# A two-layer trunk on one core: sums of h's blocks between the plain products, and the second product's pools laid out anew

## The chip, the cores and the metric

The kernel runs on one core of a Trainium2 chip. The core has five engines with a queue of instructions each: TensorE (PE: matrix products; its weight loads are listed as PEld), VectorE (DVE), ScalarE (ACT), GpSimd (POOL) and SyncE (SP, which here only issues transfers). Each queue runs in order; the engines wait for each other by semaphores. Transfers between memory and the on-chip SBUF run on 16 DMA engines, which the queues of SP and POOL feed. The metric is the device time of one execution in microseconds.

## The reference

One sequence of 1024 tokens, width 1024, two layers. Each layer modulates its input with a shift, scale and gate worked out from a vector c ("adaLN"), applies a token mixer, and then an MLP with squared ReLU:

```python
for i in range(DEPTH):                       # 2 layers
    mod = c_act @ ada_w[i] + ada_b[i]        # adaLN: 6 x 1024 columns
    shift_t, scale_t, gate_t, shift_c, scale_c, gate_c = ...
    h = rmsnorm(x, norm_g[i, 0]) * (1.0 + scale_t) + shift_t
    y = gla_mixer(h, ...) if i == 0 else diff_mixer(h, ...)
    x = x + gate_t * y
    h = rmsnorm(x, norm_g[i, 1]) * (1.0 + scale_c) + shift_c
    y = jnp.square(jax.nn.relu(h @ mlp_w1[i])) @ mlp_w2[i]   # 1024 -> 4096 -> 1024
    x = x + gate_c * y
return rmsnorm(x, final_g)
```

Layer 0 mixes with gated linear attention, layer 1 with differential softmax attention. All numbers are float32.

## The kernel before

Activations lie transposed: features on the 128 partitions, tokens in the free dimension, which is cut into two halves of 512 tokens. `x[k][half]` is block k (of 8) of the residual, `h[k][half]` the normed block. A float32 product is done in three passes: `split` (L113) makes a rounded copy `hi` on ScalarE (L114) and the rest `lo` on VectorE (L115), and `mm3` (L117) issues hi x hi, hi x lo and lo x hi. So every weight and every block of h costs one cast and one subtraction, and a block of 128 x 512 outputs from 1024 inputs is 24 matmuls.

A layer's second part is `stretch`, which runs `inner` (L762) and then `outer` (L908).

`inner` does the output projection, adds it to x, norms it, and then the MLP's first product. Output columns come in blocks n of 128. Blocks 0 to 3 are done plainly, for half 0 and then half 1 (L788 to L794): 24 matmuls, a squared ReLU (`squared`: L755 on ScalarE, L757 on VectorE), and a store to `hs` in memory (L760, issued by SP). Behind them stand the "sums of h's blocks" (L799 to L815). The remaining 28 blocks are done two at a time by `pair` (L855) with seven products instead of eight: h is seen as a 2 x 2 grid (blocks 0 to 3 and 4 to 7, half 0 and half 1), and four of the products take sums of its quarters. The sums are four VectorE subtractions for each k (L803 to L806) and four splits, three into tiles `tq` and the last (for product 4) into tiles of h. The weights of a pair are loaded as `raw` (L830) and `raw2` (L831); `ws` are their sums (L835 to L840), each split again. `part`, `sum`, `inner` are the tiles in which the products are put together (L862, L871).

`outer` is the MLP's second product, in eight parts c of 512 inner rows. A part has its weights, eight tiles `inner` loaded back from `hs` by `load_inner` (L926) and split, 12 matmuls for each of the 8 x 2 output blocks, and a residual add into x (L718). Before it all of x is loaded again (`load_x`, L728). In layer 0 it also works out the adaLN of layer 1: `ada_products` (L208) loads eight pieces of 256 KB (issued by POOL, L213; three buffers `ada_raw`) and accumulates them on VectorE (L216, L218) in one of two buffers `ada_acc`; in the next part `ada_sums` (L222) transposes them on TensorE (L226) and reduces them (L229). Twelve such products are needed, two are issued in each of the parts 0 to 5.

The order of the instructions on each engine is set by the framework's scheduler from the program and its dependences; only inside the two mixers is TensorE's order written out. On SP and on POOL transfers keep the order in which they are scheduled. Tiles come from pools that are stacked from the left or the right end of SBUF; with `reuse_waits="tile"` a new tile waits only for the tiles whose space it takes. Where a pool lies therefore decides what its first loads wait for: `raw2` and `ws` stand in the pool `st1`, over tiles of x that the sums read; the x of `outer` stands on the right, over `st1`; and the first tiles of layer 1's attention (`qk`, `v`, L1027) stand on the right, over that x.

Of the kernel before, what the change touches and what calls it, by code (L numbers as in the profile page):

```python
# [10 lines left out]
F32 = mybir.dt.float32  # L11
F32R = mybir.dt.float32r
# [4 lines left out]
ALU = mybir.AluOpType  # L17
# [4 lines left out]
P = 128  # L22
D = 1024
T = 1024
KT = D // P
HT = 512
# [56 lines left out]
def trunk(ctx: ExitStack, tc, a, out):  # L83
    nc = tc.nc
    pe, act, dve, pool = nc.tensor, nc.scalar, nc.vector, nc.gpsimd
# [5 lines left out]
    hp = ctx.enter_context(tc.tile_pool(name="hp", bufs=2 * KT))  # L91
# [3 lines left out]
    xs = dram.tile([KT, P, T], F32, name="xs")  # L95
# [17 lines left out]
    def split(hi, lo, src):  # L113
        act.copy(out=hi, in_=src)  # L114
        dve.tensor_tensor(out=lo, in0=src, in1=hi.bitcast(F32), op=ALU.subtract)  # L115
# [21 lines left out]
    def wcols(w, c0, n, pinned=False):  # L137

        return weight(w.rearrange("(k p) n -> p k n", p=P)[:, :, c0:c0 + n], [P, KT, n], pinned)
# [102 lines left out]
    def gla_v(hd, i, pinned=False):  # L242
# [12 lines left out]
    h = [[(hp.tile([P, HT], F32R, name="h_hi", tag="hhi"), hp.tile([P, HT], F32R, name="h_lo", tag="hlo"))]  # L255
         for _ in range(KT)]
# [6 lines left out]
    with tc.tile_pool(name="xa", bufs=4, reuse_waits="tile") as xa, \  # L263
# [47 lines left out]
        for j in range(4):  # L311
            t = xa.tile([P, D], F32, name="xt", tag="xt")
# [8 lines left out]
        for blk in range(4):  # L321
            c0 = blk * 256
            acc = pro2.tile([P, 2, 256], F32, name="acc", tag="acc")
            for kq in range(2):
# [3 lines left out]
                for i in range(4):  # L328
                    k = 4 * kq + i
# [23 lines left out]
            st = gp2.tile([P, 4], F32, name="st", tag="tr", bufs=2)  # L353
# [30 lines left out]
    with gla as g:  # L384
# [292 lines left out]
        h = new_h()  # L677
# [44 lines left out]
    def load_x(x, xp, halves, queue=nc.sync):  # L722
        for half in reversed(halves):
            for k in range(KT):
                x[k][half] = xp.tile([P, HT], F32, name=f"x{k}_{half}")
        for half in halves:
            for k in range(KT):
                queue.dma_start(out=x[k][half], in_=xs[k, :, half * HT:(half + 1) * HT])  # L728
# [33 lines left out]
    def inner(l, h, w_o, x, early, g, sm, tp, ps, acc_tile):  # L762
# [20 lines left out]
        h = h2  # L783

        w1 = a["mlp_w1"][l]
        ws = [wcols(w1, n * P, P) for n in range(4)]
        for half in range(2):
            for n in range(4):  # L788
                pt = acc_tile()
                for k in range(KT):  # L790
                    mm3(pt, ws[n][0][:, k, :], ws[n][1][:, k, :], *h[k][half], k == 0, k == KT - 1)
                r = tp.tile([P, HT], F32, name="relu", tag="t")
                squared(r, pt, True)
                store_inner(n, half, r)  # L794


        K2 = KT // 2
        ops = {1: [h[k][0] for k in range(K2)], 2: [h[k + K2][0] for k in range(K2)],
               3: [h[k + K2][1] for k in range(K2)], 4: [], 5: [], 6: [], 7: []}  # L799
        for k in range(K2):  # L800
            x11, x12, x21, x22 = x[k][0], x[k][1], x[k + K2][0], x[k + K2][1]
            t3 = tp.tile([P, HT], F32, name="t3", tag="t")
            dve.tensor_tensor(out=t3, in0=x22, in1=x12, op=ALU.subtract)  # L803
            dve.tensor_tensor(out=x12, in0=x12, in1=x11, op=ALU.subtract)
            dve.tensor_tensor(out=x22, in0=x22, in1=x12, op=ALU.subtract)
            dve.tensor_tensor(out=x21, in0=x21, in1=x22, op=ALU.subtract)  # L806
            for n, src in ((6, x22), (5, x12), (7, t3), (4, x21)):
                if n == 4:
                    t = (hp.tile([P, HT], F32R, name="h_hi", tag="hhi"), hp.tile([P, HT], F32R, name="h_lo", tag="hlo"))
                else:  # L810
                    t = [tq.tile([P, HT], F32R, name="tq", tag=f"t{n}{i}") for i in range(2)]
                split(t[0], t[1], src)
                ops[n].append(t)
        px.close()
        if early:  # L815
            early.close()
        st = g.enter_context(tc.tile_pool(name="st1", bufs=2, side="right", reuse_waits="tile"))

        def part(raw, shape):
# [5 lines left out]
        def pair_weights(n):  # L825

            src = w1.rearrange("(k p) n -> p k n", p=P)
            r1 = wraw.tile([P, KT, P], F32, name="raw", tag="raw")
            r2 = st.tile([P, KT, P], F32, name="raw2", tag="raw2")
            nc.sync.dma_start(out=r1, in_=src[:, :, n * P:(n + 1) * P])  # L830
            nc.sync.dma_start(out=r2, in_=src[:, :, (n + 1) * P:(n + 2) * P])  # L831
            lo_, hi_ = slice(0, K2), slice(K2, KT)
            x0 = part(r1, [P, KT, P])
            sa = st.tile([P, KT, P], F32, name="ws", tag="ws")
            dve.tensor_tensor(out=sa[:, hi_], in0=r2[:, lo_], in1=r2[:, hi_], op=ALU.add)  # L835
            dve.tensor_tensor(out=sa[:, lo_], in0=sa[:, hi_], in1=r1[:, lo_], op=ALU.subtract)
            x1 = part(sa, [P, KT, P])
            sb = st.tile([P, KT, P], F32, name="ws", tag="ws")
            dve.tensor_tensor(out=sb[:, lo_], in0=r1[:, lo_], in1=r2[:, lo_], op=ALU.subtract)
            dve.tensor_tensor(out=sb[:, hi_], in0=r1[:, hi_], in1=sa[:, lo_], op=ALU.subtract)  # L840
            x2 = part(sb, [P, KT, P])
            x3 = part(r2[:, hi_], [P, K2, P])
            return {1: (x0, 0), 2: (x0, K2), 6: (x1, 0), 5: (x1, K2), 7: (x2, 0), 3: (x2, K2), 4: (x3, 0)}
# [63 lines left out]

    def outer(l, ada_todo, after, g, tp, ps, acc_tile):  # L908

        xp = g.enter_context(tc.tile_pool(name="xp", bufs=1, side="right", reuse_waits="tile"))  # L910
        hid = g.enter_context(tc.tile_pool(name="hid", bufs=4, reuse_waits="tile"))
        sg = g.enter_context(tc.tile_pool(name="sg", bufs=3 if ada_todo else 5, reuse_waits="tile"))
        ga = g.enter_context(tc.tile_pool(name="ga2", bufs=2, reuse_waits="tile")) if ada_todo else None
        sm = g.enter_context(tc.tile_pool(name="sm2", bufs=2, reuse_waits="tile"))
        x = [[None, None] for _ in range(KT)]
        load_x(x, xp, range(2))
        add = residual(l, x)
        w2 = a["mlp_w2"][l]
        parts = FF // 512

        def load_inner(c):
            hd = [[None, None] for _ in range(4)]
            for half in range(2):
                for f in range(4):
                    raw = sg.tile([P, HT], F32, name="inner", tag="inner")
                    nc.sync.dma_start(out=raw, in_=hs[4 * c + f, :, half * HT:(half + 1) * HT])  # L926
                    if c % 2:
                        t = [hid.tile([P, HT], F32R, name="hd", tag=f"hd{half}{i}") for i in range(2)]
                    else:
                        t = [hp.tile([P, HT], F32R, name=f"h_{n}", tag=f"h{n}") for n in ("hi", "lo")]  # L930
                    split(t[0], t[1], raw)
                    hd[f][half] = t
            return hd

        sums = []
        hd = load_inner(0)
        for c in range(parts):
            ws = [weight(w2.rearrange("(f p) n -> p f n", p=P)[:, 4 * c:4 * c + 4, n * 256:(n + 1) * 256],
                         [P, 4, 256]) for n in range(4)]
            last = c == parts - 1  # L940
            now, hd = hd, None if last else load_inner(c + 1)
            for half, cols in ((0, slice(0, HT)), (1, slice(0, 256)), (1, slice(256, HT))) if last else \
                    ((0, slice(0, HT)), (1, slice(0, HT))):
                w = cols.stop - cols.start
                finish = after(half, cols, x, tp, sm, ps, acc_tile) if last else None
                for n in range(KT):
                    pt = acc_tile()[:, :w]
                    wh, wl = ws[n // 2]
                    c0 = (n % 2) * P
                    for f in range(4):  # L950
                        pe_last = mm3(pt, wh[:, f, c0:c0 + P], wl[:, f, c0:c0 + P],
                                      *(t[:, cols] for t in now[f][half]), f == 0, f == 3)
                    if half and n < len(sums):
                        with tc.issue_after(pe_last.ins):
                            ada_sums(*sums[n], ps)
                    add(n, half, pt, cols, 5)
                    if last and n == 4:
                        next(finish)
                for _ in finish or ():
                    pass  # L960
            sums = [(*todo, 512, ada_products(*todo, 512, ga, ga, pool, 2)) for todo in ada_todo[:2]]
            del ada_todo[:2]
            assert not (c >= parts - 2 and ada_todo)

    h1 = []
# [393 lines left out]
```

## Time and profile before

| | |
|---|---|
| time, median of 3 runs | 2523.32 us (2523.2 to 2525.15) |
| the profiled execution | 2523.76 us |
| its span in the profile | 2522.0 us |
| mean granted clock of TensorE | 0.977 |
| busy: PE, PEld, DVE | 2390.8 us (95%), 2055.2 (81%), 1679.3 (67%) |
| busy: ACT, POOL | 993.2 (39%), 200.5 (8%) |
| chain that ended last | PE 68%, issue 17%, DVE 7%, DMA 5%, ACT 3% |

The span is the time from the first to the last instruction that the profiler saw; the execution's own time holds a little more at its ends. Busy shares are over the whole span, though the stages have different limits. The granted clock is the share of TensorE's full clock (2.4 GHz) that it was given; 0.5 is 1.2 GHz. A wait is the idle time of an engine in front of an instruction, put down to what released it last.

### The profile page before, as it was taken

The numbers are of one execution on the slowest core, as the hardware profiler recorded it, in microseconds if no ns is written. First come the engines' busy times: TensorE is split into PE (matmuls) and PEld (weight loads), VectorE is DVE, ScalarE is ACT, GpSimd is POOL, SyncE is SP. The second block draws the span as 40 slices with busy tenths as digits, with TensorE's granted clock in tenths as the row PEclk, the third lists the DMA queues.
The fourth block names the chain that finished last, engine by engine and source line by source line (L and its number), as shares of the span: only waits on it lengthen the run. The fifth ranks groups of instructions, "written<-read, shape, count | busy, mean of one in ns | idle before, by whom it ended". The sixth has DMA issues, their size and how long they took to land.

```text
span 2522.0 us, 33385 instructions
## 1 busy us (share of the span) xinstructions
PE 2390.8 (95%) x12215; PEld 2055.2 (81%) x12215; DVE 1679.3 (67%) x3191; ACT 993.2 (39%) x1969; POOL 200.5 (8%) x354
## 2 busy tenths in 40 slices
PE   6899999979999899999899999999969999999998
PEld 5688878867888688888799999987758888788887
DVE  7777767657665576775587787788666665655444
ACT  5655555433333221212455555564443333322111
POOL 2011100000000111210121121110000000000000
PEclk8999999999999899999899999999989999999999
DMA  8333354514333755641111111024514333833211
GB/s 287 121 109 117 105 159 131 158 46 122 117 100 101 267 190 174 212 155 61 59 49 39 36 34 34 24 88 128 157 56 124 101 116 101 275 101 98 71 54 67
DMA packets 270116, 286.57 MB, mean 114 GB/s; under 512 B 15546, under 2 KB 200032, under 8 KB 269952
## 3 DMA queue, kind: packets, MB, share of 16 engines
q1 hardware_dynamic: 255552, 240.24, 29.9%
q0 software_dynamic: 12992, 41.97, 5.2%
q8 instruction: 96, 1.57, 0.3%
q10 hardware_dynamic: 1408, 2.24, 0.2%
q14 instruction: 68, 0.56, 0.1%
HBM read 222.52 MB, written 61.87 MB: 113 GB/s over the span
## 4 chain that ended last, share of the span: by engine, by line
PE 68%; issue 17%; DVE 7%; DMA 5%; ACT 3%; POOL 0%; SPq 0%; DVEq 0%; POOLq 0%; ACTq 0%
PE acc L119 12%; PE acc L118 12%; PE acc L120 12%; PE acc L851 3%; PE acc L853 3%; PE acc L852 3%; DMA ada_raw<-in_ada_w 3%; PE pp L118 3%; PE pp L120 3%; PE pp L119 3%; PE pr L118 1%; PE pr L119 1%; ACT et L1107 1%; PE pr L120 1%; PE at L1137 1%
## 5 line engine op out<-in xcount | busy, mean ns | idle before, releaser
L114 ACT CAST whi<-raw 128x1024 fp32r<-128x1024 f32 (+3 forms) x217 | 209.0, 965 | 485.1 <-PE acc L119 249.7
L718 DVE SCALAR_TENSOR_TENSOR x<-acc,mod,x 128x512 f32<-128x512 f32 (+1 forms) x312 | 222.5, 720 | 218.5 <-PE acc L120 217.5
L118 PE MATMUL acc<-h_hi,whi 128*128 128x512 f32 x896 | 353.1, 395 | 7.1 <-ACT h_hi L114 4.2
L119 PE MATMUL acc<-h_lo,whi 128*128 128x512 f32 x896 | 352.0, 393 | 6.3 <-DVE h_lo L115 6.3
L120 PE MATMUL acc<-h_hi,wlo 128*128 128x512 f32 x896 | 351.3, 393 | 0.0
L115 DVE TENSOR_TENSOR wlo<-raw,whi 128x1024 fp32r<-128x1024 f32 (+3 forms) x217 | 243.0, 1121 | 82.9 <-ACT whi L114 79.2
L118 PE MATMUL acc<-hd,whi 128*128 128x512 f32 (+1 forms) x576 | 211.8, 368 | 1.2 <-DVE x L718 1.2
L119 PE MATMUL acc<-hd,whi 128*128 128x512 f32 (+1 forms) x576 | 210.7, 366 | 0.0
L120 PE MATMUL acc<-hd,wlo 128*128 128x512 f32 (+1 forms) x576 | 210.6, 366 | 0.0
L118 PEld LDWEIGHTS acc<-h_hi,whi 128*128 128x128 f32 x896 | 169.3, 189 | 44.0 <-ACT h_hi L114 6.1
L119 PEld LDWEIGHTS acc<-h_lo,whi 128*128 128x128 f32 x896 | 169.7, 189 | 42.1 <-DVE h_lo L115 8.2
L120 PEld LDWEIGHTS acc<-h_hi,wlo 128*128 128x128 f32 x896 | 169.7, 189 | 35.3
L118 PE MATMUL pp<-whi,h_hi 128*128 128x384 f32 x512 | 184.0, 359 | 6.2 <-DVE v L115 6.2
L851 PE MATMUL acc<-h_hi,whi 128*128 128x512 f32 x448 | 175.2, 391 | 0.0
L852 PE MATMUL acc<-h_lo,whi 128*128 128x512 f32 x448 | 175.2, 391 | 0.0
L853 PE MATMUL acc<-h_hi,wlo 128*128 128x512 f32 x448 | 174.0, 389 | 0.0
L120 PE MATMUL pp<-whi,h_lo 128*128 128x384 f32 x512 | 173.6, 339 | 0.0
L119 PE MATMUL pp<-wlo,h_hi 128*128 128x384 f32 x512 | 173.3, 338 | 0.0
L851 PE MATMUL acc<-tq,whi 128*128 128x512 f32 x336 | 132.0, 393 | 38.0 <-ACT whi L114 38.0
L213 POOL DMA_DIRECT2D ada_raw<-in_ada_w x160 | 85.9, 537 | 985.3 <-PE acc L853 488.8
L218 DVE SCALAR_TENSOR_TENSOR ada_acc<-ada_raw,cact,ada_acc 128x512 f32<-128x512 f32 x140 | 104.8, 749 | 49.8 <-DMA ada_raw<-in_ada_w 48.7
L853 PE MATMUL acc<-tq,wlo 128*128 128x512 f32 x336 | 131.6, 392 | 0.1
(1800 smaller groups left out, 5188.8 us busy)
## 6 DMA issues: line engine op xcount, KB each, us to landing
raw<-in_mlp_w SPq DMA_DIRECT2D x128, 512.0 KB, 4.4
ada_raw<-in_ada_w POOLq DMA_DIRECT2D x160, 256.0 KB, 3.4
inner<-hs SPq DMA_DIRECT2D x128, 256.0 KB, 3.9
hs<-inner SPq DMA_DIRECT2D x112, 256.0 KB, 2.5
x<-xs SPq DMA_DIRECT2D x64, 256.0 KB, 5.8
raw<-in_gla_w_in SPq DMA_DIRECT2D x24, 512.0 KB, 3.9
xs<-x SPq DMA_DIRECT2D x48, 256.0 KB, 2.6
raw<-in_diff_w_in SPq DMA_DIRECT2D x64, 192.0 KB, 2.8
```

The costliest lines, as they stand in the source:

```text
L114: act.copy(out=hi, in_=src)
L115: dve.tensor_tensor(out=lo, in0=src, in1=hi.bitcast(F32), op=ALU.subtract)
L118: pe.matmul(out=o, lhsT=lh, rhs=rh, start=start, stop=False)
L119: pe.matmul(out=o, lhsT=lh, rhs=rl, start=False, stop=False)
L120: return pe.matmul(out=o, lhsT=ll, rhs=rh, start=False, stop=stop)
L213: queue.dma_start(out=w, in_=a["ada_w"][l].rearrange("(k p) n -> p k n", p=P)[:, k:k + kk, c0:c0 + n])
L218: dve.scalar_tensor_tensor(out=acc, in0=w[:, j, :], scalar=cact[:, k + j:k + j + 1], in1=acc, op0=ALU.mult, op1=ALU.add)
L718: return dve.scalar_tensor_tensor(out=t, in0=psum, scalar=mcols(l, gate)[:, kt:kt + 1], in1=t, op0=ALU.mult, op1=ALU.add)
L851: pe.matmul(out=pt, lhsT=lh, rhs=rh, start=begin and k == 0, stop=False, skip_group_check=True)
L852: pe.matmul(out=pt, lhsT=lh, rhs=rl, start=False, stop=False, skip_group_check=True)
L853: pe.matmul(out=pt, lhsT=ll, rhs=rh, start=False, stop=k == K2 - 1, skip_group_check=True)
L1107: act.activation(out=et[:, n * HT:n * HT + wn], in_=p[:, :wn], func=AF.Exp, bias=nm, scale=DH ** -0.5, accum_out=ssum[:, s, n:n + 1])
```

## The change

1. The sums of block k (three of its four splits with them) become a function, `sums_of`, called ahead of the plain product k of half 1. The splits for product 4 stay behind the plain products.
2. `raw2` and `ws` move to a pool `sw` of their own, which lies under `st1`.
3. In `outer`, x moves to the left side, and the adaLN tiles and the loads of `inner` to the right, over `sw` and `st1`. The x tiles are loaded between the two halves of part 0's inner tiles, behind the part's weights.
4. The adaLN products are issued as 0, 3, 3, 2, 2, 2, 0, 0 in parts 0 to 7, not 2, 2, 2, 2, 2, 2, 0, 0.

```diff
         for half in range(2):
             for n in range(4):
+                if half:
+                    sums_of(n)
                 pt = acc_tile()
...
+        def sums_of(k):
+            x11, x12, x21, x22 = x[k][0], x[k][1], x[k + K2][0], x[k + K2][1]
+            t3 = tp.tile([P, HT], F32, name="t3", tag="t")
+            dve.tensor_tensor(out=t3, in0=x22, in1=x12, op=ALU.subtract)
+            dve.tensor_tensor(out=x12, in0=x12, in1=x11, op=ALU.subtract)
+            dve.tensor_tensor(out=x22, in0=x22, in1=x12, op=ALU.subtract)
+            dve.tensor_tensor(out=x21, in0=x21, in1=x22, op=ALU.subtract)
+            for n, src in ((6, x22), (5, x12), (7, t3)):
+                t = [tq.tile([P, HT], F32R, name="tq", tag=f"t{n}{i}") for i in range(2)]
+                split(t[0], t[1], src)
+                ops[n].append(t)
...
         for k in range(K2):
-            for n, src in ((6, x22), (5, x12), (7, t3), (4, x21)):
...
+            t = (hp.tile([P, HT], F32R, name="h_hi", tag="hhi"), hp.tile([P, HT], F32R, name="h_lo", tag="hlo"))
+            split(t[0], t[1], x[k + K2][0])
+            ops[4].append(t)
...
+        sw = g.enter_context(tc.tile_pool(name="sw", bufs=2, side="right", reuse_waits="tile"))
         st = g.enter_context(tc.tile_pool(name="st1", bufs=2, side="right", reuse_waits="tile"))
...
-            r2 = st.tile([P, KT, P], F32, name="raw2", tag="raw2")
+            r2 = sw.tile([P, KT, P], F32, name="raw2", tag="raw2")
...
-        xp = g.enter_context(tc.tile_pool(name="xp", bufs=1, side="right", reuse_waits="tile"))
+        xp = g.enter_context(tc.tile_pool(name="xp", bufs=1, reuse_waits="tile"))
...
+        ga = g.enter_context(tc.tile_pool(name="ga2", bufs=2, side="right", reuse_waits="tile")) if ada_todo else None
+        sg = g.enter_context(tc.tile_pool(name="sg", bufs=3 if ada_todo else 5, side="right", reuse_waits="tile"))
...
-        load_x(x, xp, range(2))
...
+        def load_inner(c, between=lambda: None):
             hd = [[None, None] for _ in range(4)]
             for half in range(2):
+                if half:
+                    between()
...
+            if c == 0:
+                hd = load_inner(0, lambda: fetch_x(0))
+                fetch_x(1)
...
-            sums = [(*todo, 512, ada_products(*todo, 512, ga, ga, pool, 2)) for todo in ada_todo[:2]]
-            del ada_todo[:2]
+            n = (0, 3, 3, 2, 2, 2, 0, 0)[c]
+            sums = [(*todo, 512, ada_products(*todo, 512, ga, ga, pool, 2)) for todo in ada_todo[:n]]
+            del ada_todo[:n]
```

What this does to the order shows at three places. The first is VectorE in layer 0 at the end of the plain products (x_0 and x_1 are half 0 and half 1 of blocks of h; the last digits tell blocks apart). Before:

```order
L115 TENSOR_TENSOR h_lo<-x_1_4432,h_hi 128x512
L757 SCALAR_TENSOR_TENSOR relu<-relu 128x512 x5
L803 TENSOR_TENSOR t_5423<-x_1_4429,x_1_4425 128x512
L757 SCALAR_TENSOR_TENSOR relu<-relu 128x512
L804 TENSOR_TENSOR x_1_4425<-x_1_4425,x_0_4433 128x512
L115 TENSOR_TENSOR tq<-t_5423,tq 128x512
L805 TENSOR_TENSOR x_1_4429<-x_1_4429,x_1_4425 128x512
L115 TENSOR_TENSOR tq<-x_1_4425,tq 128x512
L806 TENSOR_TENSOR x_0_4437<-x_0_4437,x_1_4429 128x512
L115 TENSOR_TENSOR tq<-x_1_4429,tq 128x512
L803 TENSOR_TENSOR t_5444<-x_1_4430,x_1_4426 128x512
```

After, from the seventh relu of the plain products to just behind the eighth (lines L795 to L798 are the former L803 to L806):

```order
L757 SCALAR_TENSOR_TENSOR relu<-relu 128x512
L796 TENSOR_TENSOR x_1_4428<-x_1_4428,x_0_4436 128x512
L115 TENSOR_TENSOR h_lo<-x_0_4437,h_hi 128x512
L797 TENSOR_TENSOR x_1_4432<-x_1_4432,x_1_4428 128x512
L115 TENSOR_TENSOR tq<-x_1_4428,tq 128x512
L798 TENSOR_TENSOR x_0_4440<-x_0_4440,x_1_4432 128x512
L115 TENSOR_TENSOR tq<-x_1_4432,tq 128x512
L115 TENSOR_TENSOR tq<-t_5445,tq 128x512
L115 TENSOR_TENSOR h_lo<-x_0_4438,h_hi 128x512
L115 TENSOR_TENSOR h_lo<-x_0_4439,h_hi 128x512
L757 SCALAR_TENSOR_TENSOR relu<-relu 128x512
L115 TENSOR_TENSOR h_lo<-x_0_4440,h_hi 128x512
```

All relus stood ahead of the sums but one; now a block's sums and splits stand between one relu and the next, and the last block's nine operations between the seventh and the eighth. SP's order at this place is as before: the eight stores of the relus, then two loads of raw2; the first of these no longer waits for VectorE itself.

The second is SP where the second product of layer 0 begins (hs<-inner are the last stores of the first product, L926 or L940 the loads of inner, L728 or L927 those of x). Before:

```order
L926 DMA inner<-hs 128x512
L760 DMA hs<-inner 128x512
L926 DMA inner<-hs 128x512 x2
L128 DMA raw<-in_mlp_w 128x4x256
L728 DMA x_0_7468<-xs 128x512
L728 DMA x_0_7469<-xs 128x512
...
L728 DMA x_1_7467<-xs 128x512
L926 DMA inner<-hs 128x512 x8
L128 DMA raw<-in_mlp_w 128x4x256
```

After:

```order
L940 DMA inner<-hs 128x512 x3
L760 DMA hs<-inner 128x512
L128 DMA raw<-in_mlp_w 128x4x256
L940 DMA inner<-hs 128x512 x3
L128 DMA raw<-in_mlp_w 128x4x256
L927 DMA x_0_7464<-xs 128x512
L927 DMA x_0_7465<-xs 128x512
...
L760 DMA hs<-inner 128x512
L927 DMA x_1_7472<-xs 128x512
...
L927 DMA x_1_7479<-xs 128x512
L940 DMA inner<-hs 128x512 x3
```

The sixteen x loads stood in one piece ahead of eight inner loads; now nine inner loads stand ahead of them and the last three stores among them. On VectorE the sixteen accumulations of the first two adaLN products begin before these last stores and end between the first residual adds, in both kernels; the first of them stands 5 rows ahead of the first product's last L757 before, 22 rows now.

The third is ScalarE where layer 1's attention begins (sq, rs_t, rstd and h_hi belong to the norm of the last 256 tokens, qk and v are copied out of PSUM for the first head's projection). Before:

```order
L174 ACTIVATE sq<-x_1_7467 128x256
L154 ACTIVATE rs_t<-rs_m 128x2
L155 ACTIVATE rstd<-rs_t 128x2
L200 ACTIVATE h_hi<-nt,mod 128x256 x2
L196 ACTIVATE nt<-nt,mod 128x256
L197 CAST h_hi<-nt 128x256
L200 ACTIVATE h_hi<-nt,mod 128x256 x2
L196 ACTIVATE nt<-nt,mod 128x256
L197 CAST h_hi<-nt 128x256
L200 ACTIVATE h_hi<-nt,mod 128x256 x2
L1027 COPY qk<-pp 128x256
L114 CAST v<-pp 128x128
```

After:

```order
L174 ACTIVATE sq<-x_1_7473 128x256
L174 ACTIVATE sq<-x_1_7474 128x256
L1045 COPY qk<-pp 128x256
L174 ACTIVATE sq<-x_1_7475 128x256
L174 ACTIVATE sq<-x_1_7476 128x256
L174 ACTIVATE sq<-x_1_7477 128x256
L114 CAST v<-pp 128x128
L174 ACTIVATE sq<-x_1_7478 128x256
L174 ACTIVATE sq<-x_1_7479 128x256
L154 ACTIVATE rs_t<-rs_m 128x2
L155 ACTIVATE rstd<-rs_t 128x2
L1045 COPY qk<-pp 128x256
```

The first copies stood behind the whole norm and now stand between its operations. On TensorE 48 matmuls of the projection stood ahead of the norm's four st matmuls, and then four bc; now 67 stand ahead of st and 8 between st and bc. POOL's order is the same in both kernels. Elsewhere PE's differs by a few dozen rows that change places at the starts of the pairs and of the second products, and by the transposes (L226), which follow the adaLN products: none in part 1, three in parts 2 and 3.

## Rows read from the trace of the kernel before

**Rows 1.** The page's first lines: the span, then busy us (share) xinstructions of each engine.
```profile
span 2522.0 us, 33385 instructions
...
PE 2390.8 (95%) x12215; PEld 2055.2 (81%) x12215; DVE 1679.3 (67%) x3191; ACT 993.2 (39%) x1969; POOL 200.5 (8%) x354
```

**Rows 2.** TensorE's waits, whole span: engine, line, releaser: us in total, times, longest.
```profile
PE acc L851 <- ACT whi L114: 38.0, 2, 19.0
...
PE acc L119 <- DVE h_lo L115: 6.3, 3, 4.3
PE pp L118 <- DVE v L115: 6.2, 1, 6.2
PE tro L534 <- DVE ot L525: 4.3, 1, 4.3
```

**Rows 3.** Stretches: us, busy (x) of PE, PEld, DVE, ACT, POOL, clock, DMA share, GB/s.
```profile
553.00:572.50 19.50, 0.79 (x4) 0.33 (x2) 19.25 (x32) 9.06 (x15) 0.00 (x0) 0.60 0.23 67
572.50:577.50 5.00, 4.66 (x11) 3.19 (x12) 4.71 (x6) 2.67 (x4) 0.00 (x0) 0.53 0.44 118
340.00:347.00 7.00, 6.79 (x24) 5.63 (x25) 6.21 (x12) 1.90 (x3) 1.15 (x2) 0.64 0.80 272
```

**Rows 4.** VectorE in time, layer 0's plain products and sums: start, us, instruction [idle before].
```profile
543.58 0.69 DVE L757 SCALAR_TENSOR_TENSOR relu<-relu 128x512 f32<-128x512 f32 x1 [4.75 <-ACT relu L755]
...
549.62 0.68 DVE L804 TENSOR_TENSOR x<-x,x 128x512 f32<-128x512 f32 x1
...
570.99 0.68 DVE L836 TENSOR_TENSOR ws<-ws,raw 128x512 f32<-128x512 f32 x1
```

**Rows 5.** SyncE's queue in time, same place: start, us, what it issued, count.
```profile
518.49 31.56 SPq L760 DMA_DIRECT2D hs<-relu  x8
556.96 10.02 SPq L831 DMA_DIRECT2D raw<-in_mlp_w  x2
```

**Rows 6.** DMA issues of 548 to 600: count, KB each, median us to landing.
```profile
raw<-in_mlp_w SPq DMA_DIRECT2D x7, 512.0 KB, 4.1
```

**Rows 7.** Stretches around layer 0's second product.
```profile
810.00:830.00 20.00, 20.00 (x90) 16.56 (x89) 9.64 (x12) 6.54 (x10) 0.00 (x0) 1.00 0.31 106
835.00:883.00 48.00, 38.20 (x145) 29.34 (x144) 31.39 (x46) 10.31 (x16) 8.58 (x16) 0.86 0.85 300
845.00:865.00 20.00, 19.25 (x84) 15.30 (x82) 10.84 (x17) 1.86 (x3) 4.41 (x9) 1.00 1.04 387
```

**Rows 8.** SyncE's queue in time, same place.
```profile
844.08 14.19 SPq L728 DMA_DIRECT2D x<-xs  x16
860.07 20.86 SPq L926 DMA_DIRECT2D inner<-hs  x8
```

**Rows 9.** ScalarE's waits of 835 to 872.
```profile
ACT h_hi L114 <- DMA inner<-hs: 27.4, 6, 18.0
```

**Rows 10.** TensorE in time at the same place of layer 1.
```profile
2155.89 0.50 PE L118 MATMUL acc<-h_hi,whi 128*128 128x512 f32 x1 [0.72 <-ACT h_hi L114]
```

**Rows 11.** The adaLN loads of 820 to 935: ns min/median/max, first and last start.
```profile
L213 POOL DMA_DIRECT2D ada_raw<-in_ada_w x28: 536/536/538, 831.1 to 935.0; - x28
```

**Rows 12.** One product's accumulations, 921.5 to 933.7: ns min/median/max, first and last start.
```profile
L218 DVE SCALAR_TENSOR_TENSOR ada_acc<-ada_raw,cact,ada_acc x7: 740/752/752, 922.4 to 932.9; 128x512 f32<-128x512 f32 x7
```

**Rows 13.** Stretches around the start of attention in layer 1.
```profile
1225.00:1240.00 15.00, 7.49 (x25) 7.22 (x26) 6.87 (x20) 5.54 (x16) 1.45 (x2) 0.54 0.00 0
1219.00:1245.00 26.00, 14.54 (x67) 13.90 (x66) 11.68 (x32) 9.13 (x27) 1.45 (x2) 0.74 0.05 15
```

**Rows 14.** ScalarE in time, same place.
```profile
1232.81 0.35 ACT L1027 COPY qk<-pp 128x256 f32<-128x256 f32 x1
```

**Rows 15.** The page's group of adaLN accumulations: busy, mean ns | idle before.
```profile
L218 DVE SCALAR_TENSOR_TENSOR ada_acc<-ada_raw,cact,ada_acc 128x512 f32<-128x512 f32 x140 | 104.8, 749 | 49.8 <-DMA ada_raw<-in_ada_w 48.7
```

**Rows 16.** DMA issues of 820 to 900.
```profile
ada_raw<-in_ada_w POOLq DMA_DIRECT2D x19, 256.0 KB, 5.5
...
x<-xs SPq DMA_DIRECT2D x16, 256.0 KB, 7.8
```

More of the change, by code (lines that the diff above doesn't have):

```diff
@@ L786, in inner @@
         ws = [wcols(w1, n * P, P) for n in range(4)]
+        K2 = KT // 2
+        ops = {1: [h[k][0] for k in range(K2)], 2: [h[k + K2][0] for k in range(K2)],
+               3: [h[k + K2][1] for k in range(K2)], 4: [], 5: [], 6: [], 7: []}
+        def sums_of(k):
[9 more added lines that the diff above has]
+                ops[n].append(t)
         for half in range(2):
             for n in range(4):
+                if half:
+                    sums_of(n)
                 pt = acc_tile()
@@ L794, in inner @@
                 store_inner(n, half, r)
-        K2 = KT // 2
-        ops = {1: [h[k][0] for k in range(K2)], 2: [h[k + K2][0] for k in range(K2)],
-               3: [h[k + K2][1] for k in range(K2)], 4: [], 5: [], 6: [], 7: []}
         for k in range(K2):
[L801 to L806, printed above, removed]
-            for n, src in ((6, x22), (5, x12), (7, t3), (4, x21)):
[L808 to L813, printed above, removed]
+            t = (hp.tile([P, HT], F32R, name="h_hi", tag="hhi"), hp.tile([P, HT], F32R, name="h_lo", tag="hlo"))
+            split(t[0], t[1], x[k + K2][0])
+            ops[4].append(t)
         px.close()
@@ L833, in pair_weights @@
             x0 = part(r1, [P, KT, P])
-            sa = st.tile([P, KT, P], F32, name="ws", tag="ws")
+            sa = sw.tile([P, KT, P], F32, name="ws", tag="ws")
             dve.tensor_tensor(out=sa[:, hi_], in0=r2[:, lo_], in1=r2[:, hi_], op=ALU.add)
@@ L837, in pair_weights @@
             x1 = part(sa, [P, KT, P])
-            sb = st.tile([P, KT, P], F32, name="ws", tag="ws")
+            sb = sw.tile([P, KT, P], F32, name="ws", tag="ws")
             dve.tensor_tensor(out=sb[:, lo_], in0=r1[:, lo_], in1=r2[:, lo_], op=ALU.subtract)
@@ L908, in outer, with fetch_x @@
     def outer(l, ada_todo, after, g, tp, ps, acc_tile):
-        xp = g.enter_context(tc.tile_pool(name="xp", bufs=1, side="right", reuse_waits="tile"))
+        xp = g.enter_context(tc.tile_pool(name="xp", bufs=1, reuse_waits="tile"))
         hid = g.enter_context(tc.tile_pool(name="hid", bufs=4, reuse_waits="tile"))
-        sg = g.enter_context(tc.tile_pool(name="sg", bufs=3 if ada_todo else 5, reuse_waits="tile"))
-        ga = g.enter_context(tc.tile_pool(name="ga2", bufs=2, reuse_waits="tile")) if ada_todo else None
         sm = g.enter_context(tc.tile_pool(name="sm2", bufs=2, reuse_waits="tile"))
+        ga = g.enter_context(tc.tile_pool(name="ga2", bufs=2, side="right", reuse_waits="tile")) if ada_todo else None
+        sg = g.enter_context(tc.tile_pool(name="sg", bufs=3 if ada_todo else 5, side="right", reuse_waits="tile"))
         x = [[None, None] for _ in range(KT)]
-        load_x(x, xp, range(2))
+        for half in range(2):
+            for k in range(KT):
+                x[k][half] = xp.tile([P, HT], F32, name=f"x{k}_{half}")
+        def fetch_x(half):
+            for k in range(KT):
+                nc.sync.dma_start(out=x[k][half], in_=xs[k, :, half * HT:(half + 1) * HT])
         add = residual(l, x)
@@ L919, in outer @@
         parts = FF // 512
-        def load_inner(c):
+        def load_inner(c, between=lambda: None):
             hd = [[None, None] for _ in range(4)]
             for half in range(2):
+                if half:
+                    between()
                 for f in range(4):
@@ L935, in outer @@
         sums = []
-        hd = load_inner(0)
+        hd = None
         for c in range(parts):
```

## Prediction

> **What bounds the kernel now.** I read the page's first lines, then TensorE's waits, then the stretches around the longest of them. PE is busy for 2390.8 of 2522.0 us [rows 1], so a change that adds no matmul can win or lose only in the other 131 us and in matmuls that run at half clock. PE's matmuls are the same before and after, and so is POOL's order; only rows of PE, DVE, ACT and SP move. The profiled execution took 2523.76 us, 1.8 us more than its span and 0.4 us more than the median of 2523.32; the sum is made against 2523.8.
>
> The waits of PE that the change can reach stand in [rows 2]: 38.0 us in two waits of 19.0 where the seven-product pairs begin (one in each layer); 6.3 us for h_lo, nearly all of it where the second product of layer 0 begins; 6.2 us for v where the attention of layer 1 begins. The 4.3 us for ot lie elsewhere and serve as a yardstick. PE's unit of work is one plain product: 24 matmuls in 5.44 us (VectorE's relu comes every 4.75 + 0.69 us in [rows 4]), or 0.227 us a matmul at full clock.
>
> **Part 1: the sums of h's blocks.** Before, all four blocks of sums and splits follow the plain products. VectorE idles 4.75 us between relus up to 543.58, begins L804 at 549.62, and is at work without a gap to L836 at 570.99, which the first weights of the pair wait for [rows 4]. In 553 to 572.5 PE is busy 0.79 us, VectorE 19.25 [rows 3]: the wait is VectorE's queue, nothing else. Then the clock is 0.53 over the next 5 us, so 4.66 us of matmuls do about 2.5 us of work [rows 3]: 2.1 us lost. That makes 19.0 + 2.1 = 21.1 us a layer, 42.2 in both.
>
> After, block k's seven VectorE operations (32 in 19.25 us [rows 3] are 0.60 each: 4.2 us) stand between relus that leave 4.75 us free, so three blocks cost nothing; the cover is the idle VectorE, and PE waits only if a relu is late enough to hold its accumulator. The order puts nine operations ahead of the last relu, 5.4 us against 4.75, so that relu comes some 0.6 us late, at about 549.6. What is late next is the weights. SP sends its stores of the relus in order and raw2's load behind the eighth [rows 5]. The load was issued at 556.96; it no longer lies over x tiles that the sums still read, and only the eighth store holds it: I put it at 550.7. Such loads landed after 4.1 us [rows 6], so at 554.8. L835, L839 and L836 follow at 0.6 each, then ScalarE's cast of twice as many columns, 1.2 if it runs at the same rate (an estimate): PE resumes at 558, not at 572.5 or later [rows 3]. It runs out at 553.6 as before, so it idles 4.4 us, and the low half needs another 0.5 or so. A wait of 4.3 us elsewhere [rows 2] was followed by 7 us at clock 0.64 [rows 3], which is 2.5 us of work lost. Left are 4.4 + 0.5 + 2.5 = 7.4 us a layer, and the gain is 13.7, in both 27.4. Bounds: the load still lands where the old issue time puts it (556.96 + 4.1 = 561.1, PE at 564.3, a loss of 10.7 + 0.5 + 2.5, a gain of 7.4 a layer), or it hides wholly (21.1). I take the middle because the store is the only wait left.
>
> **Part 2: the pools of the second product, layer 0.** In 835 to 883 PE is busy for 38.2 of 48 us and starts 145 matmuls [rows 7]: 9.8 us idle and, since 145 x 0.227 is 32.9, up to 15.1 in all. I count 14. SP issues sixteen loads of x from 844.08 and the eight inner loads behind them only from 860.07 [rows 8]; ScalarE waits up to 18.0 us for inner [rows 9]; in 845 to 865 the DMA engines are full, 387 GB/s at a share of 1.04, while 810 to 830 ran at 0.31 [rows 7]. The same place in layer 1, with the same x loads and no adaLN loads, shows a wait of 0.72 us [rows 10].
>
> After, nine inner loads stand ahead of x in SP's queue, and x, which needs no space of the pairs' weights any more, goes out between the last hs stores. The adaLN loads do not move later here: part 0 asks for none now, but part 1's stand in VectorE's order even sooner, since their tiles lie over raw2 and ws, free once the last pair's weights are split. I estimate 15 to 25 us, three to five products, before the 831.1 of [rows 11]. Inner is in place when PE arrives; the next things late are x (now issued some 10 us sooner than 844.08, and first needed when PE has done a whole product) and adaLN data. I expect a loss of 1, near layer 1's 0.72: a gain of 13. Bounds: 0 and 14; below 0 is rival D.
>
> The Trainium skill ("DMA: Bandwidth & Descriptors", section "Issuing engines are not separate DMA queues") says that transfers started by different engines run on the same sixteen DMA engines. By that rule alone reordering SP's queue moves no bytes and the gain would be nothing; the trace agrees that the engines are shared (share 1.04, [rows 7]) but shows 0.31 in the 20 us ahead, so the sum keeps its 13.
>
> **Part 3: three adaLN products in parts 2 and 3.** adaLN accumulators have two buffers, so the third product's eight accumulations begin only after the first one's transposes, and PE's order puts its own transposes some 46 matmuls later, 10.4 us. Behind an L216 of half a us, seven L218 took from 922.4 to 932.9 + 0.75 [rows 12], eight in 11.7 us. PE would stand still for 1.3 us, perhaps with a half-clock stretch of the size in [rows 3] behind it. Twice, that is 2.6 to 7.6, and as little as 0 if VectorE, whose eight accumulations alone are 8 x 0.75 us, does them sooner; I take 3. Transposes dropped from part 0 cost nothing either way.
>
> **Part 4: the start of attention.** In 1219 to 1245 PE is busy for 14.54 of 26 us, and of that 7.49 us lie in 1225 to 1240 at a clock of 0.54 [rows 13]: 11.5 idle and 3.4 lost to the clock, 14.9. The cause is on ScalarE: qk's copy out of PSUM stands at 1232.81 behind the whole norm [rows 14], because its target lay over x. Before, PE's queue had 48 projection matmuls ahead of the norm's st. After, x lies on the other side, the copies stand between the norm's operations, and PE has 67 ahead of st, 8 between st and bc: 27 matmuls of 384 columns, 27 x 0.227 x 384/512 = 4.6 us of work, move into the norm's waits (11.5 less the 6.2 for v [rows 2] is 5.3), and the 6.2 us vanish because the two PSUM buffers are emptied in time. Left: 1.5, no half clock. Gain 13.4; bounds 0 and 14.9.
>
> Layer 1's second product, 0.72 before, may gain that or lose as much. All stages behind these four are bound by PE, so a gain here is not given back later.
>
> **Sum.** 2523.8 - 27.4 - 13 + 3 - 13.4 = 2473.0.
>
> **Rivals.**
> A. raw2 still gates. SP is in order, and the 10.02 us that two such loads held it [rows 5] speak for a queue that doesn't move; against it, what held it were the sums. Then part 1 gives 14.8, not 27.4: 2486.
> B. The DMA engines stay the limit in part 2: sixteen x and sixteen adaLN loads of 256 KB must still pass. The 1.04 speaks for it, the 0.31 ahead against. Part 2 gives 0: 2486. If part 4 gives nothing instead (the copies late again behind the norm's own waits): 2486 too.
> C. No rest anywhere: raw2 hides and part 3 costs nothing: 2473 - 14.8 - 3 = 2455. Against: SP's eighth store.
> D. Slower. VectorE is in order, and sixteen adaLN accumulations now stand between the last pair's sums and the splits of inner. Each waits for its load, and everything behind it with it. Before, such accumulations waited 48.7 us for their loads in the whole kernel, 0.35 us each over 140 [rows 15]. To eat the 51 us and be 5 slower, each of the sixteen must cost PE 3.5 us more than now: 2529. The loads that feed them have an emptier DMA than before, and PE's queue has a pair's 12-matmul products as cover. Also under D: the adaLN loads don't start "a part later" at all, so what the change says of them isn't what it does.
>
> The Trainium skill ("SBUF — State Buffer", section "SBUF: two separate sides") warns that transfers issued from POOL stall while VectorE runs certain two-port operations, because their descriptors can't be written. [...] The trace gives it little: in 820 to 900 POOL's adaLN loads landed after a median of 5.5 us, SP's x loads of the same size after 7.8 [rows 16].
>
> **How the numbers follow.** The forecast, 2463 to 2483, has 0.56; A, 0.14; B in either place or both (2486 to 2499), 0.18; C, 0.07; D, 0.03; and 0.02 for a result within 5 us of before, by several smaller failures. 5 us, 0.2%, is what a measurement here can tell from no change. The range 2461 to 2494 leaves out most of C, D and both places of B. Faster 0.95, same 0.02, slower 0.03.
>
> **What would show it.** After the plain products PE should idle 3 to 6 us in both layers, with relus and sums alternating on VectorE and raw2 issued near 550. In layer 0's second product inner must be issued ahead of x, and ScalarE's 18 us wait must be gone. At the attention's start, near 1195 after the gains ahead of it, the copies must stand between norm operations and the clock hold 1.0. New waits of a few us should be at L226 in parts 2 and 3. I am wrong if raw2 lands after 560, if PE waits behind adaLN operations of VectorE for more than a few us, or if the attention's first copies still follow the norm.

## The result

The changed kernel takes 2477.44 us (median; 2476.71 to 2478.59), the kernel before 2523.26 in the same comparison: 0.9819 of its time, with a 95% interval of 0.9802 to 0.9836. Forecast were 2473, with a range of 2461 to 2494. In the comparison with e10 and e11 one execution of e10 and one of the kernel before took twice as long and longer; they are left out. The profiled execution took 2476.71 us, with a span of 2474.9 us, 47.1 less than before.

Its page, the same two lines as in [rows 1]:

```profile
span 2474.9 us, 33402 instructions
...
PE 2385.8 (96%) x12215; PEld 2052.2 (83%) x12215; DVE 1680.7 (68%) x3191; ACT 990.8 (40%) x1969; POOL 201.4 (8%) x354
```

PE does the same matmuls; its busy time fell by 5 us, since fewer of them run at half clock, and the other 42 us were waits. What PE waits for now, of the whole span, as in [rows 2]:

```profile
PE acc L856 <- ACT whi L114: 9.8, 2, 5.0
PE ada_st L226 <- DVE mod L229: 6.9, 1, 6.9
...
PE ada_st L226 <- DVE ada_acc L218: 2.4, 2, 1.8
```

The waits at the pairs' start fell from 38.0 to 9.8 us. Those for h_lo and v of [rows 2] are gone. New are three at L226, the adaLN transposes, 9.3 us together.

**Start of the pairs.** SP's queue and VectorE in time, which answer to [rows 5] and [rows 4] (L840 is the former L835, L836 the former L831):

```profile
518.15 32.22 SPq L760 DMA_DIRECT2D hs<-relu  x8
550.42 1.17 SPq L836 DMA_DIRECT2D raw<-in_mlp_w  x2
```

```profile
549.34 0.69 DVE L757 SCALAR_TENSOR_TENSOR relu<-relu 128x512 f32<-128x512 f32 x1
...
553.58 0.69 DVE L876 TENSOR_TENSOR sum<-acc,part 128x512 f32<-128x512 f32 x1 [2.96 <-PE acc L858]
555.28 0.69 DVE L840 TENSOR_TENSOR ws<-raw 128x512 f32<-128x512 f32 x1 [1.01 <-DMA raw<-in_mlp_w]
```

raw2 goes out at 550.42, right behind the eighth store, and L840 waits for it until 555.28. PE ran out at 553.47 and waited 4.84 us:

```profile
558.30 0.80 PE L856 MATMUL acc<-tq,whi 128*128 128x512 f32 x1 [4.84 <-ACT whi L114]
```

Stretches, with columns as in [rows 3]:

```profile
558.00:563.00 5.00, 4.66 (x10) 3.26 (x11) 5.00 (x7) 2.77 (x4) 0.00 (x0) 0.50 0.60 167
785.00:805.00 20.00, 20.00 (x90) 16.57 (x89) 9.72 (x12) 6.89 (x11) 1.60 (x3) 1.00 0.45 144
805.00:825.00 20.00, 19.58 (x87) 15.84 (x86) 18.31 (x28) 9.13 (x15) 3.77 (x7) 1.00 0.93 319
825.00:845.00 20.00, 20.00 (x90) 16.57 (x89) 11.58 (x18) 3.35 (x6) 4.84 (x9) 1.00 1.04 394
1184.00:1215.00 31.00, 30.06 (x202) 29.22 (x201) 25.87 (x69) 17.82 (x47) 2.56 (x4) 1.00 0.37 120
```

In 558 to 563 PE works at a clock of 0.50 and so loses 2.3 us, about what it lost there before (2.1).

**Start of the second product.** Before, 810 to 830 ran at a DMA share of 0.31 and the crowd came when the product had begun [rows 7]; now it begins on PE near 823, and the DMA engines are at 0.93 from 805 and at 1.04 from 825, with PE busy for 59.58 of the 60 us. The transfers are as crowded as they were, but the crowd starts earlier. SP's queue, which answers to [rows 8]:

```profile
812.57 2.78 SPq L940 DMA_DIRECT2D inner<-hs  x3
...
818.05 0.97 SPq L927 DMA_DIRECT2D x<-xs  x2
...
828.00 6.27 SPq L927 DMA_DIRECT2D x<-xs  x8
```

Inner is ahead of x. **Start of attention:** PE is busy for 30.06 of 31 us in 1184 to 1215 at full clock, where [rows 13] had 14.54 of 26. ScalarE's copies, which answer to [rows 14], now stand between the norm's operations:

```profile
1200.70 0.35 ACT L1045 COPY qk<-pp 128x256 f32<-128x256 f32 x1
...
1201.91 0.40 ACT L174 ACTIVATE sq<-x 128x256 f32<-128x256 f32 x1
...
1203.24 0.35 ACT L1045 COPY qk<-pp 128x256 f32<-128x256 f32 x1
```

**The new wait.** The longest one at L226 is in part 4 of the second product, counted from 0 as in the plan (the expectation of e10 below counts from 1 and calls it part 5). TensorE, then VectorE and SP around it:

```profile
1027.03 0.60 PE L226 MATMUL ada_st<-ident,ada_acc 128*128 128x128 f32 x4
...
1037.33 1.11 PE L226 MATMUL ada_st<-ident,ada_acc 128*128 128x128 f32 x4 [6.95 <-DVE mod L229]
```

```profile
1018.11 1.22 DVE L115 TENSOR_TENSOR wlo<-raw,whi 128x1024 fp32r<-128x1024 f32 x1
...
1024.56 0.75 DVE L218 SCALAR_TENSOR_TENSOR ada_acc<-ada_raw,cact,ada_acc 128x512 f32<-128x512 f32 x1 [1.33 <-DMA ada_raw<-in_ada_w]
1025.23 0.69 DVE L115 TENSOR_TENSOR h_lo<-inner,h_hi 128x512 fp32r<-128x512 f32 x1
...
1030.65 1.51 DVE L115 TENSOR_TENSOR h_lo<-inner,h_hi 128x512 fp32r<-128x512 f32 x2 [2.12 <-ACT h_hi L114]
...
1034.66 0.69 DVE L115 TENSOR_TENSOR h_lo<-inner,h_hi 128x512 fp32r<-128x512 f32 x1 [1.24 <-ACT h_hi L114]
...
1036.59 0.68 DVE L229 TENSOR_REDUCE mod<-ada_st 128x4 f32<-128x512 f32 x1
```

```profile
1005.26 7.47 SPq L940 DMA_DIRECT2D inner<-hs  x4
1019.35 0.38 SPq L128 DMA_DIRECT2D raw<-in_mlp_w  x1
1021.93 13.77 SPq L940 DMA_DIRECT2D inner<-hs  x8
```

The four transposes take PSUM space that the reduce L229 has to read first. L229 runs at 1036.59, because ahead of it on VectorE stand splits of inner tiles that wait for ScalarE's casts, and these for loads that SP issues from 1021.93 on. SP in turn waits for VectorE. It stood at a load of weights until 1019.35, whose buffer the split at 1018.11 had to free. Then its inner loads wait for splits that free the inner buffers: the first goes out at 1021.93, the second only behind the split at 1025.23, for which SP waits 3.6 us. That split stands behind an adaLN accumulation, which waits 1.33 us for its own load. The loads start 5.1 us ahead of the part's first transposes at 1027.03. The granted clock is 0.50 for some 6.8 us from the last part of the wait on; PE works in 3.8 of them, which costs 1.9 more: 9.3 + 1.9 = 11.2 us for part 3 of the forecast.

### The profile page after: what moved, and what is told of

The parts are those of the page before. It is cut to its first block, busy times and chain, and to the rows that moved or that the text cites. A ratio compares the mean times of both kernels' runs of the same rounds, so it can differ in the third digit from the quotient of the medians.

```text
span 2474.9 us, 33402 instructions
## 1 busy us (share of the span) xinstructions
PE 2385.8 (96%) x12215; PEld 2052.2 (83%) x12215; DVE 1680.7 (68%) x3191; ACT 990.8 (40%) x1969; POOL 201.4 (8%) x354
## 4 chain that ended last, share of the span: by engine, by line
PE 72%; issue 11%; DMA 7%; DVE 6%; ACT 3%; POOL 1%; SPq 0%; DVEq 0%; POOLq 0%; ACTq 0%
PE acc L118 10%; PE acc L119 10%; PE acc L120 10%; PE acc L856 7%; PE acc L857 7%; PE acc L858 7%; DMA ada_raw<-in_ada_w 5%; PE pp L118 3%; PE pp L120 3%; PE pp L119 3%; PE at L1155 1%; PE pr L118 1%; PE pr L119 1%; PE pr L120 1%; PE bc L164 1%
```

## The experiments

Each is timed beside the kernel before on one chip, and the ratio is to that; the brackets hold its 95% interval.

**adaLN in twos (e1).**

```diff
-            n = (0, 3, 3, 2, 2, 2, 0, 0)[c]
+            n = (2, 2, 2, 2, 2, 2, 0, 0)[c]
```

> The changed kernel with adaLN products again 2, 2, 2, 2, 2, 2, 0, 0 over the parts. The changed kernel takes 2477.4 us and shows waits at the transposes of 0.6, 1.8 and 6.9 us, the last followed by 6.8 us at half clock: about 12 in all. Theory: these come from three products in a part (VectorE's queue is longer, the weights' splits and with them SP's loads of inner come late); with two in each they go, and the time is 2465 (2463 to 2468). Rival: they come from the new place of the inner tiles and their loads, whatever the plan of adaLN; then at least the 6.9 us and its half clock stay, 2475 to 2478.

2465.42 us, 0.9775 (0.9760 to 0.9789). No wait at L226 is left. SP's queue at the same place, where the weights' load no longer stands late, and TensorE's first transposes of the part:

```profile
1008.50 0.38 SPq L128 DMA_DIRECT2D raw<-in_mlp_w  x1
1009.82 10.98 SPq L940 DMA_DIRECT2D inner<-hs  x8
```

```profile
1022.32 0.60 PE L226 MATMUL ada_st<-ident,ada_acc 128*128 128x128 f32 x4
```

Here the eight loads start 12.5 us ahead of the first transposes, not 5.1, and no accumulation stands between the splits that free their buffers: the last one begins at 1004.73, 17.6 us ahead of the transposes, where in the changed kernel it begins 2.5 us ahead. So 11 to 12 us of what the change gains elsewhere are lost by its own plan of adaLN.

**One part with three products (e10)**, `(1, 3, 2, 2, 2, 2, 0, 0)`:

> The changed kernel with adaLN 1, 3, 2, 2, 2, 2, 0, 0: one part with three products, not two. In the changed kernel the long wait (6.9 us) stands in part 5, where a reduce on VectorE is queued behind splits of inner tiles whose loads SP issued late, behind a weights' load that waited for VectorE. Theory: each third product adds eight accumulations to a part's VectorE queue, and the long wait is the backlog of two such parts; with one there is at most a wait of 0.5 to 2 us at the transposes behind it: 2465 to 2468. Rival: one third product is enough to bring VectorE and SP into that late order, and it stays: 2473 to 2478.

2466.74 us, 0.9777 (0.9756 to 0.9798): the theory. All of PE's waits at L226:

```profile
PE ada_st L226 <- DVE ada_acc L218: 0.4, 1, 0.4
```

One third product, in part 1, costs a wait of 0.4 us; the long wait came only with a second one in part 2. Whether the number counts or the place isn't tested: no run has its third product in part 2 alone.

**Transposes later (e5)**, on the plan of the changed kernel:

```diff
-                    if half and n < len(sums):
+                    if half and 0 <= n - 4 < len(sums):
                         with tc.issue_after(pe_last.ins):
-                            ada_sums(*sums[n], ps)
+                            ada_sums(*sums[n - 4], ps)
```

> The changed kernel (adaLN 0, 3, 3, 2, 2, 2) with a part's transposes behind the products n = 4, 5, 6 of half 1, not 0, 1, 2. Theory: PE comes to the transposes before VectorE is through, with the accumulations in two cases and with a reduce that stands behind late splits of inner in the third; 10.9 us later all three waits are gone: 2466 (2464 to 2469). Rival: VectorE is simply too long in these parts, and the third product, which starts behind the first transposes, now ends later still; its waits move into the next part, and the time stays at 2474 to 2480.

2474.81 us, 0.9806 (0.9787 to 0.9825): the theory fell. The waits moved along with the transposes, PE's again:

```profile
PE ada_st L226 <- DVE mod L229: 6.6, 1, 6.6
PE ada_st L226 <- DVE ada_acc L218: 1.3, 2, 0.8
```

Coming later doesn't help, since the accumulations behind the first transposes come later too. The picture of the forecast, that PE comes to the transposes before VectorE is through, is right for the small waits (2.4, now 1.3 us) and wrong for the large one.

How the lateness reaches part 4 can be read from VectorE's accumulations. There are two accumulator buffers, and the products run one behind the other. In the changed kernel the third product of part 2's plan runs from 981.75 to 993.07. In e10 the first of the next two products stands there (982.36 to 994.20). So in the changed kernel these two begin 14 us later, at 996.55, and end at 1025.31, among the splits that free SP's buffers; in e10 they end at 1007.61.

**The sums alone (e2)**: the kernel before with `sums_of` between the plain products, raw2 and everything else where it was.

> The kernel before with the sums of h's blocks between the plain products, and no pool moved. Theory: VectorE's queue was the wait, so nearly all of part 1 comes from the order of the sums: 27 us less than before, 2496 (2494 to 2499), with two waits of 5 us at the pairs' start. Rival: raw2's place over x still holds its load, until the last cast or split of x (0.6 to 3 us later in each layer, and half clock with it): 2499 to 2505. If the place of raw2 is what counted: 2523.

2493.80 us, 0.9887 (0.9872 to 0.9902): the theory, with 28.5 us (0.2 us under its range). PE's waits, and SP's queue at the pairs' start:

```profile
PE acc L854 <- ACT whi L114: 9.8, 2, 5.0
...
PE pp L118 <- DVE v L115: 6.2, 1, 6.2
PE acc L119 <- DVE h_lo L115: 5.8, 3, 3.8
```

```profile
550.15 1.13 SPq L834 DMA_DIRECT2D raw<-in_mlp_w  x2
```

The pairs' two waits are as short as in the changed kernel, the other two of [rows 2] about as long as before. raw2 goes out as early as in the changed kernel, though it lies where it lay: its new place has no part in it.

**raw2 past the store (e6)**, on the changed kernel:

```diff
-            nc.sync.dma_start(out=r2, in_=src[:, :, (n + 1) * P:(n + 2) * P])
+            (pool if n < 8 else nc.sync).dma_start(out=r2, in_=src[:, :, (n + 1) * P:(n + 2) * P])
```

> The changed kernel with the first two raw2 loads of each layer issued by POOL, so that they stand behind no store. Theory: SP's eighth store is what still holds raw2; without it raw2 lands before 551, L840 follows the last sums, and of the wait of 4.8 us and the 6.8 us at half clock little is left in either layer: 2463 to 2468. Rival: the three VectorE operations and the cast (3.0 us from L840 to PE's start) and the space of the last x tiles hold it as long: at most 1.7 us a layer, 2474 to 2477.

2472.84 us, 0.9808 (0.9789 to 0.9827), with two waits of 3.7 us left of 4.8 and 5.0. The time lies 1 us under the rival's range and 5 above the theory's, and the waits tell for the rival. The time alone tells little: in this run's profile the long wait at L226 is 3.3 us, not 6.9, and the edit gives no direct reason for that. POOL's queue, and VectorE behind it:

```profile
533.63 0.91 POOL L836 DMA_DIRECT2D raw<-in_mlp_w  x1 [191.47 <-ACT tq L114]
544.56 0.89 POOL L836 DMA_DIRECT2D raw<-in_mlp_w  x1 [10.02 <-DVE h_lo L115]
```

```profile
552.89 0.69 DVE L876 TENSOR_TENSOR sum<-acc,part 128x512 f32<-128x512 f32 x1 [2.96 <-PE acc L858]
553.50 0.68 DVE L840 TENSOR_TENSOR ws<-raw 128x512 f32<-128x512 f32 x1
```

raw2 is issued 17 us sooner and, since such loads landed after a median of 4.8 us, is in place long before 549. Still L840 comes at 553.50, since ahead of it in VectorE's queue stands the first pair's sum L876, which waits 2.96 us for PE's second product. The store had hidden a second gate, that is, a second thing that holds L840.

**Weights ahead of the sum (e8)**: adaLN in twos, raw2 by POOL, and that sum issued behind the split of the first ws (`ready[n]` is the subtraction in it; the lines for the other two are left out).

```diff
             product(pb, w, 2, True)
-            done(n, 0, pb, s1)
+            with tc.issue_after(ready[n].ins):
+                done(n, 0, pb, s1)
```

> The changed kernel with adaLN 2 in each of parts 0 to 5, the first two raw2 loads of a layer issued by POOL, and on VectorE the first sum of a pair (L876, which waits for PE's second product) put behind the pair's first ws and its split. In the run with POOL's loads raw2 had been issued at 533.6 and L840 still stood behind that sum until 553.5, while VectorE idled 3 us. Theory: this sum is what is left of the wait at the pairs' start; L840 now runs at 550 and PE's waits of 3.7 us and their half clock go, so the time is 2450 (2447 to 2455). Rival: PE then waits for the low halves of the weights (a cast of 1.05 and a subtraction of 1.2 each) and still falls to half clock: 2457 to 2463.

2455.50 us, 0.9731 (0.9708 to 0.9755): faster than both kernels, by 22 us than the changed one, of which adaLN in twos gives 11 to 12. It is 0.5 us above the theory's range, and the rival's half clock didn't come. VectorE and TensorE at the pairs' start, and a stretch with columns as in [rows 3]:

```profile
550.77 0.68 DVE L842 TENSOR_TENSOR ws<-raw 128x512 f32<-128x512 f32 x1
...
556.65 0.68 DVE L879 TENSOR_TENSOR sum<-acc,part 128x512 f32<-128x512 f32 x1
```

```profile
553.79 0.50 PE L859 MATMUL acc<-tq,whi 128*128 128x512 f32 x1
...
555.05 0.50 PE L861 MATMUL acc<-tq,wlo 128*128 128x512 f32 x1 [0.53 <-DVE wlo L115]
```

```profile
553.00:558.50 5.50, 4.49 (x17) 2.44 (x15) 5.11 (x7) 3.15 (x4) 0.00 (x0) 1.00 0.38 105
```

L842 (the former L840) runs at 550.77; PE goes on with a pause of 0.53 us for the low half, and its clock stays at 1.00.

**The order without POOL (e11)**: e8 with raw2 issued by SP.

> The run with POOL's raw2 loads and the sum behind the first ws and its split (2455.5), but with raw2 issued by SP again, behind the eighth store. Theory: both the store and the sum's place hold the first ws, and each alone is worth little; raw2 lands at 555, L840 starts there, and 2 to 3 us of wait with half clock stay in each layer: 2462 to 2466, close to the 2465.4 of adaLN in twos alone. Rival: the sum's place was all, and the time is 2455 to 2458.

2465.62 us, 0.9774 (0.9758 to 0.9789), no gain over e1's 2465.42. VectorE waits for raw2 again:

```profile
553.92 0.69 DVE L842 TENSOR_TENSOR ws<-raw 128x512 f32<-128x512 f32 x1 [4.43 <-DMA raw<-in_mlp_w]
```

Of the two gates, taking away the store's alone leaves 7.5 of the 9.8 us of PE's two waits (e6), and the sum's alone leaves 9.6 and gains no time (e11); both together take the waits away and gain 10 us (e8 against e1).

**The second product's pools alone (e3)**: the kernel before with the changed `outer` and adaLN in twos, without `sw`.

> The kernel before with only the second product's pools and loads as in the changed kernel, adaLN 2 in each of parts 0 to 5. SP has x partly ahead of inner here. Theory that the early place of x and of inner (free of the pairs' last tiles) is what part 2 gained, and that the left place of x is what part 4 gained: 15 + 14 + 1.5 us less than before, 2493 (2490 to 2496). Rival: the order of inner ahead of x is what counted in part 2, so its 10 us wait stays here, and only part 4's gain shows: 2506 (2503 to 2510).

2526.83 us, 1.0015 (1.0005 to 1.0024): no faster than before, at most 0.24% slower, and neither theory. PE's waits, and SP's queue in layer 0:

```profile
PE acc L118 <- ACT h_hi L114: 22.4, 3, 11.1
...
PE acc L119 <- DVE h_lo L115: 4.2, 1, 4.2
```

```profile
830.27 0.46 SPq L922 DMA_DIRECT2D x<-xs  x1
...
841.09 1.56 SPq L935 DMA_DIRECT2D inner<-hs  x3
```

Without `sw` the tiles of inner lie over `st1`, the last pair's own results, so they are loaded from 841 on, behind eleven of the sixteen x loads, while PE is through by 836. It waits 11 us in both layers; layer 1 had lost under 1. Attention's start gained all the same: PE's waits there (1180 to 1260) are 1.8 us, 12.7 before (1190 to 1250).

**The same with sw (e9)**: the sums left where they were.

> The kernel before with the pool sw for raw2 and ws and the second product's pools and loads of the changed kernel, adaLN 2 in each of parts 0 to 5, and the sums of h's blocks where they were. The same without sw came to 2526.8, with waits of 11 us for h_hi at the start of the second product in both layers. Theory: inner must not lie over the pairs' last tiles (st1) but over weights that are read sooner, which is what sw is for; then parts 2 and 4 give 15 + 14 + 1.5 us: 2493 (2490 to 2497), with no wait over 1 us at the start of the second product and two waits of 19 us at the pairs' start. Rival: the early end of the pairs' sums is needed too, and part of the 11 us waits stays: 2500 to 2515.

2495.16 us, 0.9889 (0.9866 to 0.9912): the theory. `sw` is worth 32 us to `outer`. SP's queue:

```profile
818.17 2.71 SPq L936 DMA_DIRECT2D inner<-hs  x3
...
829.66 0.97 SPq L923 DMA_DIRECT2D x<-xs  x2
```

Inner is loaded from 811 on, over the space of weights that are split sooner, and x behind it.

## Why the prediction was right

By its own terms, against the trace:

- **Part 1, 27.4 forecast.** The two waits fell by 28.2 us. The loss to the clock is 2.3 against 2.1 us in layer 0 and some 3 against 2.3 in layer 1, so 27 to 28 us as forecast; e2 gave 28.5 in time. raw2 was put at 550.7 and its landing at 554.8; it was issued at 550.42, and L840 ended its wait at 555.28. The half-clock stretch after a wait of 4.84 us came as the yardstick of 4.3 us had it. One reason was wrong without harm: raw2's new place was to free its load, but e2 has the same waits without it. And "the store is the only wait left" was wrong: e6 showed L876 behind it.
- **Part 2, 13.** The whole loss of about 14 went, down to a wait of 0.4 us: 13.6. The order in SP's queue was named as the cause; e3 and e9 show that the gain hangs on the place of inner's tiles over `sw`, which the forecast didn't name, and that the new places of x and inner without it cost what they give.
- **Part 3, -3.** This is the step that failed: it measured 11.2 us, and 11 to 12 by e1, above its own upper bound of 7.6. The waits that it worked out came in parts 2 and 3, with 0.6 and 1.8 us near the 1.3 forecast for each and without half clock. The wait of 6.9 us in part 4, where only two products are transposed, stands in no term. The forecast left out that accumulations delay what stands behind them on VectorE: the splits that free SP's next loads, and a reduce of another product. So one of its signs of being wrong came, PE behind an adaLN operation of VectorE for more than a few us.
- **Part 4, 13.4.** 14.0: what is left is one wait of 0.9 us at full clock.
- Layer 1's second product gained its 0.95 us, no more.

The sum of the trace is 28.2 + 13.6 - 11.2 + 14.0 + 0.95 = 45.5 of 47.1. Part of the rest is that part 2's loss was more than 14. At the start of layer 0's second product the changed kernel is 13.5 us ahead (836.36 against 822.84 for its first matmul), and at that product's last wait 17.3 (1199.05 against 1181.72). So parts 2 and 3 gained 3.8 us together, and with -11.2 part 2 comes to 15.0, near the upper count of the forecast (15.1). Missing part 3 by 8 us and gaining some 4 in the others makes the 4 us by which the forecast was short. That the total came so close is in part luck, since these errors have opposite signs.

Of the rivals, A (raw2's load still goes out late) and B (the DMA engines stay full) didn't come; by the rule cited from the Trainium skill ("DMA: Bandwidth & Descriptors", "Issuing engines are not separate DMA queues") the engines stay shared, and the trace agrees (a share of 1.04 in 825 to 845). But the crowd now starts ahead of the loads' use, and the gain was not nothing. C's conditions, raw2 hidden and no cost of part 3, hold in e8, with its time (2455.50 against 2455). Of the Trainium skill's warning of POOL's transfers beside VectorE's work ("SBUF — State Buffer", "SBUF: two separate sides") the trace shows nothing: in 785 to 850 the adaLN loads landed after a median of 5.5 us, as in [rows 16]. D was right in its kind and wrong in its place: accumulations in VectorE's queue did hold PE up, not at the start of the second product but in its part 4.

## What to carry to other kernels

A queue that runs in order hides its second gate behind the first: of the two things that held the first weights, removing one gave a quarter of the waits or nothing, and only both together all. When work is added to an engine with slack, price what stands behind it in the queue, not only what it feeds: here PE waited for a reduce behind splits, these for loads, and the loads for another split's buffer. A pool's neighbours decide what a load waits for: the same layout of `outer` gained nothing over one pool and 28 us over another.

## What the runs showed of the hardware

DMA engines at a share of 1.04 (394 GB/s) in 825 to 845 did PE no harm, while the same share in 845 to 865 of the kernel before [rows 7] lay in a stretch with a loss of 14 us: the two differ in which transfers stood first.

PE's granted clock fell to 0.50, 1.2 GHz, in or behind the waits of 3.7 to 5.0 us at the pairs' start and the 6.9 us at L226. It stayed at 1.00 behind the wait of 1.84 us that ended at 993.21 in the changed kernel, and was down to 0.53 in 839.8 to 843.3 of the kernel before, behind a wait of 1.84 us too. So the length of a wait alone doesn't tell.
